# Two edits of a one-core encoder layer: a tail whose last quarter is centred early and summed by TensorE, and an attention head scaled by POOL

## The chip, the cores and the metric

The kernel runs on one core of one Trainium2 chip. The metric is the device time of one execution in microseconds (us). A core has five engines that this text names: PE (TensorE, matmuls into PSUM), DVE (VectorE, elementwise work), ACT (ScalarE, activations, with a free scale, bias and row sum), POOL (GpSimd, elementwise work from SBUF to SBUF, and DMAs of its own queue) and SP (a queue that issues DMAs). Each engine executes its own list of instructions in order and waits on semaphores for the others. POOL cannot read PSUM.

## The reference, cut to what matters

One layer on 1024 prompt rows and 32 sample rows, 1024 features. The parts that the change touches are the softmax of the sparse attention, and the second layer norm.

```python
logits = jnp.where(valid[:, :, None, None, :], logits + bias, NEG)
p = jax.nn.softmax(logits, axis=-1)
out = jnp.einsum('btgrk,btkgd->btgrd', p, v_sel)
...
hid = jax.nn.relu(x @ w_ff1)
ff = (hid * hid) @ w_ff2
x = _layernorm(ALPHA * x + ff, ln2_g, ln2_b)

def _layernorm(x, g, b):
    mu = jnp.mean(xf, axis=-1, keepdims=True)
    xc = xf - mu
    var = jnp.mean(xc * xc, axis=-1, keepdims=True)
    y = xc * lax.rsqrt(var + LN_EPS) * g + b
```

## The kernel before, in words

Everything is held with features on the 128 partitions and rows of x (1056 of them) along the free dimension. A product of two f32 matrices is made of three matmuls on a high and a low part (lines 875 to 877 in the feed-forward part, 131 to 133 elsewhere), so every weight tile is loaded, split by ACT (L108, high part) and POOL or DVE (L111, low part), and then multiplied. The order of a run is: input projections, indexer scores and the top-k search; attention and the output projection (about 350 to 545 us of the profile); first layer norm and feed-forward products by a Strassen-like scheme (seven products instead of eight, on halves of 528 rows); the last of these products, the second layer norm, and the output.

**Attention.** `PLAN` lists nine query tiles `t` of 128 rows (one of 32), each with four pairs of heads `g2`. For a pair, `att_softmax` multiplies queries with keys and adds the position bias (L572 to L576, PE), adds the mask and takes the row minimum of the negated logits on DVE (L578, one instruction for each chunk of up to 512 keys, each followed by a read of the accumulator), joins the minima of two chunks (L583, DVE), takes the exponential with its row sum (L584, ACT), the reciprocal (L586, DVE), and scales the two heads: head 0 by DVE (L587), head 1 by ACT (L588). `att_values` then transposes the result in tiles of 128 (L606, PE) and multiplies with the values (L620 to L623). Six `L` tiles let three pairs be under way. POOL meanwhile makes low parts of weights (`whl`, L111) and of attention outputs (`area`, L111), and issues the loads of the queries `q` (L521), each of which waits until PE has read the buffer it writes. Other jobs, such as parts of the output projection and of the first layer norm, are put between the pairs. A scheduler decides the order on every engine in this stage.

**The tail.** From the feed-forward part on the order is written out by hand: `run` goes through a list of `Step`s and emits for each its loads, preparations, matmuls (`mm`) and what follows (`post`), on all engines in that order. A `plain` step is 12 matmuls (four weight tiles, three matmuls each) into one PSUM tile, and one DVE addition of it to a tile of z (L1288). A quarter `q` of the rows (264) has eight plain steps, one for each feature tile `d`. `M5` and `M3` are steps of two of the seven products. The order of the end is `qs[0] + qs[1] + M5 + M3[0] + qs[2] + M3[1] + qs[3]`. Four PSUM tiles `acc` rotate through all of these. Ahead of `qs[0]` stand the steps `P4`, whose four results are added to z by DVE (L1028), and 12 `fold`s (L1035) add kept partial sums `u` to z, eight on DVE and four on POOL.

**Second layer norm.** The quarters 0 to 2 go through `ln2_parts`: three sums over tiles on POOL (L1254), the mean by a matmul with a matrix of 1/1024 (`small_sum`, L1233; one such f32 call is two MATMUL records in the trace), centring on DVE (L1262), squares on ACT (L1264, L1267) and their sums on POOL (L1268), the root (L1273, ACT) and its reciprocal (L1274, DVE), scaling of the four z tiles (L1239) by the engine that the table at the end names, and scale and shift on ACT with the store (L1244, L1245). The last quarter has its own function, `last_quarter`: after two plain steps it takes a rough offset (`offset`, a sum over two tiles), subtracts it from each tile (L1305, tiles 0 to 3 on DVE after their product, 4 to 7 on POOL before it), squares each tile (L1310, ACT), and keeps two running sums, of the tiles and of the squares, on DVE (L1312 and L1313, each 128 x 264). At the end PE forms mean and variance of these sums (L1233), and the tiles are centred exactly (L1341, DVE and POOL), scaled (L1239, three on DVE and one on POOL), finished on ACT (L1244) and stored.

## Time and profile before

| | |
|---|---|
| median of 3 runs | 1309.21 us (1307.82 to 4234.3) |
| the profiled execution | 1309.35 us |
| its span, first to last instruction | 1307.0 us |
| PE busy | 1231.6 us, 94% |
| DVE busy | 963.6 us, 74% |
| ACT busy | 694.1 us, 53% |
| POOL busy | 584.0 us, 45% |

The span is the time between the first and the last instruction in the trace, and the profiled execution's own time is 2.35 us above it. The page gives for each engine how long it was busy, the chain of work that ended last, and the costliest groups of instructions. In the views that are used here, "idle" before an instruction is the time in which its engine had nothing to do just before it, with the instruction that ended the wait behind an arrow. Matmuls overlap, so the distance from one start to the next tells their cost and not their length. PEclk is the clock that TensorE was granted, where 1.00 is the full one.

### The profile page before, as it was taken

Reading aid. Unit: us, or ns where it says so; the run is one execution under the profiler, and the core shown is the slowest. Engines: PE = TensorE matmul, PEld = TensorE weight load, DVE = VectorE, ACT = ScalarE, POOL = GpSimd, SP = SyncE. Lnnn points to the kernel's source line nnn. Section 1 sums busy time; section 2 is a strip of 40 time slices with the busy share of each in tenths; the row PEclk is TensorE's granted clock in tenths of the full one; section 3 lists DMA queues with packets and bytes.
Section 4 is the critical chain, followed back from the end, with each engine's and each line's share of the span. In section 5 each row is a group of like instructions: output and inputs, shape, how many; then the busy total and the mean of one; then the engine's idle time right before and its main releaser. Section 6 shows DMA issues by size and latency. Waiting matters only on the chain. (4 is left out here: it accounts for less than half of the span.)

```text
span 1307.0 us, 24077 instructions
## 1 busy us (share of the span) xinstructions
PE 1231.6 (94%) x8846; PEld 1194.1 (91%) x8846; DVE 963.6 (74%) x1986; ACT 694.1 (53%) x1370; POOL 584.0 (45%) x463
## 2 busy tenths in 40 slices
PE   7999999998899998799799999999899999998994
PEld 6999999988898987788799999999899999998993
DVE  5675799999579988877857667576647667577666
ACT  5666989843698888784322222221344444444244
POOL 2412355423521252374544453544444444448764
PEclk9999999998999999999899999999999999999996
DMA  6321111125631231243134344443873563553112
GB/s 207 100 72 38 34 49 50 49 100 168 172 89 20 49 73 33 65 157 122 43 124 161 119 157 147 143 164 126 283 276 93 178 203 108 163 170 118 34 51 84
DMA packets 97222, 149.98 MB, mean 115 GB/s; under 512 B 12456, under 2 KB 41808, under 8 KB 97104
## 3 DMA queue, kind: packets, MB, share of 16 engines
q1 hardware_dynamic: 81664, 139.55, 32.9%
q0 software_dynamic: 9504, 4.33, 2.0%
q10 hardware_dynamic: 5936, 4.58, 1.2%
q8 instruction: 69, 1.13, 0.4%
q14 instruction: 49, 0.40, 0.1%
HBM read 105.41 MB, written 43.00 MB: 114 GB/s over the span
## 5 line engine op out<-in xcount | busy, mean ns | idle before, releaser
L111 POOL TENSOR_TENSOR whl<-wraw,whl 128x512 fp32r<-128x512 f32 (+1 forms) x184 | 253.5, 1382 | 413.1 <-ACT whl L108 391.1
L875 PE MATMUL acc<-b,whl 128*128 128x264 f32 x1088 | 310.0, 285 | 5.8 <-DVE ring L954 2.7
L876 PE MATMUL acc<-b,whl 128*128 128x264 f32 x1088 | 310.1, 285 | 0.0
L877 PE MATMUL acc<-b,whl 128*128 128x264 f32 x1088 | 308.6, 284 | 0.0
L875 PEld LDWEIGHTS acc<-b,whl 128*128 128x128 f32 x1088 | 204.8, 188 | 6.8 <-DVE ring L954 2.9
L108 ACT ACTIVATE whl<-wraw 128x512 fp32r<-128x512 f32 (+1 forms) x184 | 113.4, 623 | 174.2 <-DVE wraw L870 141.9
L877 PEld LDWEIGHTS acc<-b,whl 128*128 128x128 f32 x1088 | 205.4, 189 | 0.0
L876 PEld LDWEIGHTS acc<-b,whl 128*128 128x128 f32 x1088 | 204.4, 188 | 0.0
L132 PE MATMUL mm<-area,whl 128*128 128x384 f32 (+4 forms) x552 | 180.6, 328 | 0.4 <-DVE area L111 0.4
L131 PE MATMUL mm<-xh,whl 128*128 128x384 f32 (+4 forms) x520 | 170.4, 329 | 9.6 <-ACT whl L108 5.6
L133 PE MATMUL mm<-xh,whl 128*128 128x384 f32 (+4 forms) x520 | 169.2, 330 | 0.4 <-POOL whl L111 0.4
L111 DVE TENSOR_TENSOR b<-xraw,b 128x528 fp32r<-128x528 f32 x94 | 69.9, 745 | 85.3 <-ACT b L108 85.2
L108 ACT ACTIVATE b<-xraw 128x528 fp32r<-128x528 f32 x94 | 60.6, 644 | 132.5 <-PE acc L877 75.0
L441 ACT ACTIVATE junka<-s,cand 128x1024 bf16<-128x1024 f32 (+1 forms) x93 | 96.4, 1036 | 31.0 <-DVE cand L454 25.5
L131 PEld LDWEIGHTS mm<-xh,whl 128*128 128x128 f32 (+1 forms) x520 | 97.1, 187 | 12.5 <-ACT whl L108 6.2
L132 PEld LDWEIGHTS mm<-area,whl 128*128 128x128 f32 (+1 forms) x552 | 103.2, 187 | 3.3 <-DVE area L111 0.8
L133 PEld LDWEIGHTS mm<-xh,whl 128*128 128x128 f32 (+1 forms) x520 | 96.9, 187 | 3.8 <-POOL whl L111 1.3
L111 POOL TENSOR_TENSOR whl<-at,whl 128x512 fp32r<-128x512 f32 x56 | 80.4, 1445 | 31.8 <-ACT whl L108 31.8
L443 DVE TENSOR_SCALAR_CACHE_REDUCE junk<-s,cand 128x384 bf16<-128x384 f32 (+1 forms) x124 | 80.2, 647 | 1.1
L875 PE MATMUL acc<-area,whl 128*128 128x264 f32 x240 | 68.6, 286 | 0.0
L877 PE MATMUL acc<-area,whl 128*128 128x264 f32 x240 | 68.1, 284 | 0.0
L876 PE MATMUL acc<-area,whl 128*128 128x264 f32 x240 | 68.0, 283 | 0.0
(323 smaller groups left out, 3327.4 us busy)
## 6 DMA issues: line engine op xcount, KB each, us to landing
hd<-ring SPq DMA_DIRECT2D x98, 264.0 KB, 2.1
xraw<-hd SPq DMA_DIRECT2D x98, 264.0 KB, 2.7
at<-in_w_dram SPq DMA_DIRECT2D x58, 256.0 KB, 3.5
wraw<-in_win_dram SPq DMA_DIRECT2D x52, 256.0 KB, 2.6
wraw<-in_wo_dram SPq DMA_DIRECT2D x40, 256.0 KB, 2.7
w_a<-in_w_dram SPq DMA_DIRECT2D x23, 256.0 KB, 3.6
w_c<-in_w_dram SPq DMA_DIRECT2D x19, 256.0 KB, 3.7
zz<-zd SPq DMA_DIRECT2D x4, 1056.0 KB, 8.7
```

What stands on the lines that cost most here:

```text
L108: S.activation(hi, raw, AF.Copy)
L111: (lo_eng or G).tensor_tensor(lo, raw, f32(hi), op=OP.subtract)
L131: PE.matmul(ps, wh[k], a, start=(k == 0), stop=False)
L132: PE.matmul(ps, wh[k], b, start=False, stop=False)
L133: PE.matmul(ps, wl[k], a, start=False, stop=(k == K - 1))
L441: S.activation(junk(R, N), s, AF.Sign, bias=c, scale=-1.0, accum_out=cnt[:R, i:i + 1])
L443: V.tensor_scalar(junk(R, N), s, c, -float(k), op0=OP.is_ge, op1=OP.add, accum_out=cnt[:R, i:i + 1])
L875: PE.matmul(ps, wh, xhi, start=start, stop=False, skip_group_check=more)
L876: PE.matmul(ps, wh, xlo, start=False, stop=False, skip_group_check=more)
L877: PE.matmul(ps, wl, xhi, start=False, stop=stop, skip_group_check=more)
```

## The change

In `att_softmax` the minimum of the second chunk starts from that of the first, so that the joining instruction goes away, and head 0 is scaled by POOL instead of DVE. In the tail, all folds go to DVE, and six of them move from `P4` into the first six steps of `qs[0]`. `last_quarter` takes its offset from tiles 4 and 5 ahead of its own products, after step 6 of `qs[2]`, and DVE subtracts it from all eight tiles, two at a time, between there and the end of `M3[1]`. DVE keeps running sums of the tiles 0 to 3 alone; PE adds these sums and each of the tiles 4 to 7 with its square into a PSUM tile `stats` (`total`, one step later than the tile, the last two after step 7). At the end DVE alone scales, and it also finishes the last two tiles. The scaling of quarter 2 goes from POOL to DVE, and its last two outputs stand behind the exact centring. The parts of quarter 1's norm stand one to four steps earlier.

```diff
@@ -575,16 +575,16 @@
                     PE.matmul(ps[:R, w - 256:w], antir[:, :R], hh[g][:, h0 + i, :], start=False, stop=False)
                     mm = PE.matmul(ps[:R, w - 256:w], antir[:, :R], hl[g][:, h0 + i, :], start=False, stop=True)
                 done["QK"] = mm
-                V.tensor_tensor_reduce(L[:, c:c + n], ps[:R, pad:pad + n], mask[:, c:c + n], -1.0, -LOWEST,
-                                       op0=OP.add, op1=OP.min, accum_out=mn[:R, i, ci:ci + 1])
+                V.tensor_tensor_reduce(L[:, c:c + n], ps[:R, pad:pad + n], mask[:, c:c + n], -1.0,
+                                       mn[:R, i, 0:1] if ci else -LOWEST, op0=OP.add, op1=OP.min,
+                                       accum_out=mn[:R, i, ci:ci + 1])
         sm = small.tile([128, 2], F32, name="sm")
         for h in range(2):
-            if len(chunks) == 2:
-                V.tensor_scalar(mn[:R, h, 0:1], mn[:R, h, 0:1], mn[:R, h, 1:2], None, op0=OP.min)
-            S.activation(ls[h], ls[h], AF.Exp, bias=mn[:R, h, 0:1], scale=-1.0, accum_out=sm[:R, h:h + 1])
+            S.activation(ls[h], ls[h], AF.Exp, bias=mn[:R, h, len(chunks) - 1:len(chunks)], scale=-1.0,
+                         accum_out=sm[:R, h:h + 1])
         rs = small.tile([128, 2], F32, name="rs")
         V.reciprocal(rs[:R], sm[:R])
-        V.tensor_scalar(ls[0], ls[0], rs[:R, 0:1], None, op0=OP.mult)
+        G.tensor_scalar(ls[0], ls[0], rs[:R, 0:1], None, op0=OP.mult)
         S.activation(ls[1], ls[1], AF.Copy, scale=rs[:R, 1:2])
         return ls
 
@@ -1291,7 +1291,9 @@
     def plain(q):
         return [plain_step(q, d) for d in range(8)]
 
-    def last_quarter():
+    last_out = []
+
+    def last_quarter(qs, M3):
 
         c0, n = H + Q, Q
         cols = slice(c0, c0 + n)
@@ -1301,58 +1303,68 @@
         def ztile(d):
             return z[d // 2][:, d % 2, cols]
 
-        def centre(d, e):
-            e.tensor_tensor(ztile(d), ztile(d), got["off"], op=OP.add)
+        def offset():
+            mid = small_sum([(ones, z[2][:, a, cols]) for a in range(2)])
+            got["off"] = n2_ring.parts[0][:, :Q]
+            S.activation(got["off"], mid, AF.Copy, scale=-4.0)
+
+        def centre(i):
+            zi = z[i][:, :, cols]
+            V.tensor_tensor(zi, zi, got["off"][:, None].to_broadcast([128, 2, n]), op=OP.add)
 
         def square(d):
-            sq = got["sq"] = unit("sqa" if d % 2 else "sqb")[:, 0]
+            sq = got[d] = n2_ring.parts[1 + d % 4][:, :Q]
+            if d == 0:
+                got["sums"] = unit("s1")
             sums = got["sums"]
             S.activation(sums[:, 1] if d == 0 else sq, ztile(d), AF.Square)
-            if 0 < d < 7:
+            if 0 < d < 4:
                 V.tensor_tensor(sums[:, 0], ztile(0) if d == 1 else sums[:, 0], ztile(d), op=OP.add)
                 V.tensor_tensor(sums[:, 1], sums[:, 1], sq, op=OP.add)
 
-        def offset():
-            mid = small_sum([(ones, z[0][:, a, cols]) for a in range(2)])
-            got["off"] = n2_ring.parts[0][:, :Q]
-            S.activation(got["off"], mid, AF.Copy, scale=-4.0)
-            for i in range(4, 8):
-                centre(i, G)
-
-        def begin(*ds):
-            if ds[0] == 0:
-                got["sums"] = unit("s1")
-            for i in ds:
-                centre(i, V)
-                square(i)
+        def total(d):
+
+            if d == 3:
+                got["stats"] = new_acc()
+            for i, a in enumerate((got["sums"][:, 0], got["sums"][:, 1]) if d == 3 else (ztile(d), got[d])):
+                PE.matmul(got["stats"][:, i], ones, a, start=(d == 3), stop=(d == 7))
 
         def end():
-            sums = got["sums"]
-            mean = small_sum([(ones, sums[:, 0]), (ones, ztile(7))])
-            var = small_sum([(ones, sums[:, 1]), (ones, got["sq"])])
+            mean, var = got["stats"][:, 0], got["stats"][:, 1]
             mean2 = unit("s2")[:, 0]
             S.activation(mean2, mean, AF.Square)
             pair = unit("rstd")
             mean1, rstd = pair[:, 0], pair[:, 1]
+            V.tensor_tensor(mean2, var, mean2, op=OP.subtract)
             S.activation(mean1, mean, AF.Copy)
-            for i in range(4):
+            S.activation(rstd, mean2, AF.Sqrt, bias=eps)
+            for i in (0, 2, 3, 1):
                 zi = z[i][:, :, cols]
                 e, m = (V, mean) if i < 2 else (G, mean1)
                 e.tensor_tensor(zi, zi, m[:, None].to_broadcast([128, 2, n]), op=OP.subtract)
                 if i == 0:
-                    V.tensor_tensor(mean2, var, mean2, op=OP.subtract)
-                    S.activation(rstd, mean2, AF.Sqrt, bias=eps)
-                if i == 1:
                     V.reciprocal(rstd, rstd)
-            for i, e in ((0, V), (3, G), (1, V), (2, V)):
-                scaled(c0, n, rstd, (i,), e)
-                out(c0, n, (i,))
-
-        steps[1].post.append(offset)
-        steps[2].post.append(lambda: begin(0, 1))
-        steps[3].post.append(lambda: begin(2, 3))
-        for d in range(4, 8):
+            for f in last_out:
+                f()
+            for i in range(4):
+                scaled(c0, n, rstd, (i,), V)
+                zi = z[i][:, :, cols]
+                for a in range(2):
+                    j = 2 * i + a
+                    g, b = lnw[:, 2, j:j + 1], lnw[:, 3, j:j + 1]
+                    if i < 3:
+                        S.activation(zi[:, a], zi[:, a], AF.Identity, scale=g, bias=b)
+                    else:
+                        V.tensor_scalar(zi[:, a], zi[:, a], g, b, op0=OP.mult, op1=OP.add)
+                    nc.sync.dma_start(yT[j * 128:j * 128 + 128, c0:c0 + n], zi[:, a])
+
+        for f, st in ((offset, qs[2][6]), (lambda: centre(2), qs[2][7]), (lambda: centre(3), M3[1][0]),
+                      (lambda: centre(0), M3[1][1]), (lambda: centre(1), M3[1][3])):
+            st.post.append(f)
+        for d in range(8):
             steps[d].post.append(lambda d=d: square(d))
+        for d in range(3, 8):
+            steps[min(d + 1, 7)].post.append(lambda d=d: total(d))
         steps[7].post.append(end)
         return steps
 
@@ -1372,14 +1384,16 @@
         steps[n + 36 + 4 * j].prep.append(prep)
     for j in range(4):
         d = (j + 3) % 4
-        P4[j].post[:0] = [fold(d, 1, 0, V), fold(d, 1, 1, G)]
-    qs = [plain(0), plain(1), plain(2), last_quarter()]
-    P4[0].post.append(fold(3, 0, 1, V))
+        P4[j].post[:0] = [fold(d, 1, 0, V)]
+    qs = [plain(0), plain(1), plain(2)]
+    P4[0].post += [fold(3, m, 1, V) for m in range(2)]
     for d in range(3):
-        P4[1 + d].post.insert(0, fold(d, 0, 1, V))
+        for m in range(2):
+            qs[0][2 * d + m].post.append(fold(d, m, 1, V))
     (load5, _, prep5, step5), (load3, make3, prep3, step3) = P5, P3
     M5 = [step5(d, (0, 1)) for d in range(4)]
     M3 = [[step3(d, (c,)) for d in range(4)] for c in range(2)]
+    qs.append(last_quarter(qs, M3))
     steps += qs[0] + qs[1] + M5 + M3[0] + qs[2] + M3[1] + qs[3]
     for j in range(4):
         if j < 3:
@@ -1394,11 +1408,14 @@
     for f, st in zip(prep3, (M5[3], M3[0][0], M3[0][1])):
         st.prep.append(f)
     for q, eng, when in ((0, G, (qs[1][2], qs[1][7], M5[3], M3[0][0], M3[0][0], M3[0][1], M3[0][2], M3[0][3])),
-                         (1, V, (M3[0][1], qs[2][5], M3[1][0], M3[1][2], M3[1][1], M3[1][2], M3[1][3], qs[3][0])),
-                         (2, G, (M3[1][1], qs[3][3], qs[3][4], qs[3][5], qs[3][5], qs[3][6], qs[3][6], qs[3][7]))):
+                         (1, V, (M3[0][1], qs[2][3], qs[2][4], qs[2][6], qs[2][6], qs[2][7], M3[1][0], M3[1][1])),
+                         (2, V, (M3[1][1], qs[3][3], qs[3][4], qs[3][5], qs[3][5], qs[3][6], None, None))):
         when = (qs[q][3], qs[q][5], qs[q][7]) + when
         for f, st in zip(ln2_parts(q * Q, Q, eng), when):
-            st.post.append(f)
+            if st is None:
+                last_out.append(f)
+            else:
+                st.post.append(f)
     with tc.manual_schedule(engines=ORDERED):
         run(steps, 3, 6)
```

Two places show how the instructions stand; names carry a buffer number behind an underscore. On DVE, in the last plain steps, from the reciprocal of quarter 2 to the last step's addition (L1288 adds a plain product, L1312 and L1313 are the running sums; zz0 to zz3 hold z, two tiles each). Before:

```order
L1274 RECIPROCAL at_7307<-at_7307 128x264
L1288 TENSOR_TENSOR zz2_10751<-acc_14352,zz2_10751 128x264
L1312 TENSOR_TENSOR w_d_11223<-w_d_11223,zz2_10751 128x264
L1313 TENSOR_TENSOR w_d_11223<-w_d_11223,at_7307 128x264
L1288 TENSOR_TENSOR zz2_10751<-acc_14371,zz2_10751 128x264
L1312 TENSOR_TENSOR w_d_11223<-w_d_11223,zz2_10751 128x264
L1313 TENSOR_TENSOR w_d_11223<-w_d_11223 128x264
L1288 TENSOR_TENSOR zz3_10783<-acc_14394,zz3_10783 128x264
L1312 TENSOR_TENSOR w_d_11223<-w_d_11223,zz3_10783 128x264
L1313 TENSOR_TENSOR w_d_11223<-w_d_11223,at_7307 128x264
L1288 TENSOR_TENSOR zz3_10783<-acc_14419,zz3_10783 128x264
```

The same stretch in the change, up to the last quarter's reciprocal (L1239 scales quarter 2, L1338 is the variance, L1344 the exact centring):

```order
L1274 RECIPROCAL at_7275<-at_7275 128x264
L1288 TENSOR_TENSOR zz2_10719<-acc_14316,zz2_10719 128x264
L1239 TENSOR_TENSOR zz0_10419<-zz0_10419,at_7275 128x2x264
L1239 TENSOR_TENSOR zz1_10452<-zz1_10452,at_7275 128x2x264
L1288 TENSOR_TENSOR zz2_10719<-acc_14336,zz2_10719 128x264
L1239 TENSOR_TENSOR zz2_10719<-zz2_10719,at_7275 128x2x264
L1239 TENSOR_TENSOR zz3_10751<-zz3_10751,at_7275 128x2x264
L1288 TENSOR_TENSOR zz3_10751<-acc_14359,zz3_10751 128x264
L1288 TENSOR_TENSOR zz3_10751<-acc_14380,zz3_10751 128x264
L1338 TENSOR_TENSOR w_d_11191<-acc_14331,w_d_11191 128x264
L1344 TENSOR_TENSOR zz0_10419<-zz0_10419,acc_14331 128x2x264
L1346 RECIPROCAL at_7275<-at_7275 128x264
```

The running sums between the additions are gone, and the four scalings of quarter 2, which POOL did, stand there. On POOL, a stretch of the attention stage around tile 2 (`area` is the low part of an attention output). Before:

```order
L521 DMA q_5368<-qd_2596 128x4x128
L521 DMA q_5554<-qd_2596 128x4x128
L111 TENSOR_TENSOR area_63<-ao_4478,area_63 128x2x128 x2
L521 DMA q_5729<-qd_2596 128x4x128
L111 TENSOR_TENSOR area_63<-ao_5044,area_63 128x2x32 x2
L521 DMA q_5907<-qd_2596 128x4x128
L111 TENSOR_TENSOR whl_5535<-wraw_5536,whl_5535 128x512
L111 TENSOR_TENSOR whl_5624<-wraw_5625,whl_5624 128x512
```

And in the change, where the same loads `q_5729`, `q_5907` are named `q_5701`, `q_5875`:

```order
L111 TENSOR_TENSOR area_63<-ao_4468,area_63 128x2x128
L587 TENSOR_SCALAR L_5172<-L_5172,rs_5197 128x768
L521 DMA q_5701<-qd_2596 128x4x128
L587 TENSOR_SCALAR L_5261<-L_5261,rs_5286 128x768
L111 TENSOR_TENSOR area_63<-ao_5028,area_63 128x2x32 x2
L587 TENSOR_SCALAR L_5351<-L_5351,rs_5376 128x768
L521 DMA q_5875<-qd_2596 128x4x128
L111 TENSOR_TENSOR whl_5511<-wraw_5512,whl_5511 128x512
L587 TENSOR_SCALAR L_5441<-L_5441,rs_5466 128x768
L111 TENSOR_TENSOR whl_5598<-wraw_5599,whl_5598 128x512
```

The scalings (L587) stand among the splits, and behind and ahead of loads that wait for PE, where POOL had only splits and loads. Of the folds, eight stand on DVE between the last two groups of L1028 before; in the change six do, and the other six stand one by one behind the first six additions L1288 of `qs[0]`, and none on POOL.

## Rows read from the trace of the kernel before

**Rows 1.** Page, part 1: busy time, share of the span, instructions.

```profile
PE 1231.6 (94%) x8846; PEld 1194.1 (91%) x8846; DVE 963.6 (74%) x1986; ACT 694.1 (53%) x1370; POOL 584.0 (45%) x463
```

**Rows 2.** Chain that ended last, its end: start us, us, what.

```profile
1266.89 0.90 PE acc L1233 x4
...
1291.54 3.90 PE acc L1233 x8
1295.46 0.43 DVE w_d L1343
...
1296.51 1.79 DVE at L1346
...
1302.32 1.99 ACT zz L1244 x4
```

**Rows 3.** Timeline of PE in the last plain steps: start, us, instruction, idle before.

```profile
1270.53 0.28 PE L875 MATMUL acc<-area,ew 128*128 128x264 f32 x1
...
1278.34 1.05 PE L1233 MATMUL acc<-w_d,cs 128*128 128x264 f32 x4
...
1284.94 0.28 PE L877 MATMUL acc<-area,ew 128*128 128x264 f32 x1
```

**Rows 4.** Timeline of DVE, ACT and POOL from 1284 us to the end.

```profile
1284.74 5.64 POOL L1239 TENSOR_TENSOR zz<-zz,at 128x528 f32<-128x528 f32 x4 [5.39 <-DVE at L1274]
...
1286.26 1.52 DVE L1313 TENSOR_TENSOR w_d<-w_d,at 128x264 f32<-128x264 f32 x1
...
1291.56 0.43 DVE L1313 TENSOR_TENSOR w_d<-w_d,at 128x264 f32<-128x264 f32 x1
1291.91 0.43 DVE L1288 TENSOR_TENSOR zz<-acc,zz 128x264 f32<-128x264 f32 x1
...
1293.43 0.41 ACT L1310 ACTIVATE w_d<-zz 128x264 f32<-128x264 f32 x1
...
1298.32 0.71 DVE L1239 TENSOR_TENSOR zz<-zz,at 128x528 f32<-128x528 f32 x1
```

**Rows 5.** Timeline of DVE at the folds, and of PE behind them.

```profile
1193.41 3.52 DVE L1035 TENSOR_TENSOR zz<-zz,w_c 128x528 f32<-128x528 f32 x2
1196.86 9.36 DVE L1035 TENSOR_TENSOR zz<-zz,w_b 128x528 f32<-128x528 f32 x6
1206.14 2.54 DVE L1028 TENSOR_TENSOR zz<-acc,zz 128x528 f32<-128x528 f32 x4
...
1206.88 0.39 PE L875 MATMUL acc<-area,ew 128*128 128x264 f32 x1 [3.41 <-DVE zz L1028]
```

**Rows 6.** Attention stage: busy time of all engines, then of L587, of L583.

```profile
350.00:545.00 195.00, 181.88 (x1226) 169.66 (x1225) 162.01 (x498) 163.88 (x368) 65.43 (x62) 0.98 0.25 62
...
350.00:545.00 195.00, 22.25 (x36) 0.98 0.25 62
...
350.00:545.00 195.00, 6.66 (x32) 0.98 0.25 62
```

**Rows 7.** Attention stage, waits of PE: us in total, times, longest.

```profile
PE qk_b L572 <- DVE mn L578: 5.7, 6, 2.8
PE tr_b L606 <- ACT L L588: 1.8, 1, 1.8
PE mm_b L131 <- DVE z L414: 1.8, 1, 1.8
PE tr_b L606 <- DVE L L587: 1.3, 1, 1.3
PE tr_b L606 <- DVE pt L614: 1.2, 3, 0.5
```

**Rows 8.** Groups by shape: busy us, mean ns of one, idle before.

```profile
L587 DVE TENSOR_SCALAR L<-L,rs 128x1024 f32<-128x1024 f32 x4 | 3.0, 751 | 0.1
...
L111 POOL TENSOR_TENSOR whl<-wraw,whl 128x512 fp32r<-128x512 f32 x182 | 251.9, 1389 | 405.8 <-ACT whl L108 383.8 <-PE qk L274 14.8 <-issue 4.1
...
L405 POOL CAST area<-ch 128x384 fp32r<-128x384 f32 x4 | 2.5, 646 | 4.4 <-PE mm L132 4.4
```

## The prediction, as it was made before the change ran

> **What bounds the kernel now.** I read the page's busy shares first. [rows 1] say that PE is busy for 94% of the span and no other engine for more than 74%. So a cut on DVE, ACT or POOL is worth something only where PE stands still for it, and the two edits have to be priced by PE's idle time in their own stages. Next I read the end of the chain of waits [rows 2], because at the end of a run PE has nothing left and every engine's delay is on the path. The reader is to see there that nothing but the sums (L1233), DVE's centring and reciprocal and ACT's scale and shift follows the products, and that the four last sums took 3.90 us where two others took 0.90, that is twice as long for each. The timelines of PE [rows 3] and of the other engines [rows 4] then show why the end starts late. The first product of `qs[3]` starts at 1270.53, which I call T0, the last one at 1284.94, but the sums wait until 1291.54, 6.5 us in which PE does nothing. DVE is the engine that is late: the addition of the last tile starts at 1291.91 because the running sums ahead of it are slow. One of them took 1.52 us at 1286.26, while POOL scaled quarter 2 (5.64 us from 1284.74), and 0.43 us at 1291.56, when POOL was still.
>
> For the fold edit I read the timelines of DVE and PE at the folds [rows 5]. Eight folds take 12.9 us on DVE, the additions of `P4` stand behind them, and PE's first plain product waits 3.41 us for one of these additions. For the attention edit I read the stage by engine [rows 6] and PE's waits in it [rows 7]: of 195 us PE is busy for 181.88, DVE for 162.01, ACT for 163.88 and POOL for 65.43. Its waits on DVE come to 5.7 + 1.8 + 1.3 + 1.2 = 10.0 us, 5.7 of them at the row minima (L578), and one wait of 1.8 on ACT's scaling.
>
> **The tail.** *Removed:* the offset's sum within `qs[3]`, six of DVE's twelve running sums, POOL's part in the scaling, and the four sums after the last addition. *Added:* five pairs of sums on PE, three of them among the plain steps, two after the last. A plain step is 12 matmuls of 0.12 us, 1.46 us, so eight are 11.7 us ([rows 3]: 14.5 us from T0 to the end of the last, with the offset's sum, a sum of quarter 2 and the waits between). A pair of f32 sums is 0.90 us at the full clock, from the x4 row of [rows 2]. The products of `qs[3]` then end at 11.7 + 0.9 (quarter 2's sum) + 3 x 0.9 = T0 + 15.3. The last addition is 0.43 us and ACT's square 0.41 [rows 4]: T0 + 16.1. Tile 6's sums lie under these; tile 7's take 0.9 more: T0 + 17.0. I take full clock here because PE now stands still for under a microsecond before them, where it stood for 6.5 us before; at the half clock they take another 0.9, and I keep that as a bound. Subtraction 0.43 [rows 2], the root and the reciprocal: the chain before has 0.43 at 1295.46 and the reciprocal's end at 1298.30, which is 2.84 us from one to the other with the centring between. The change keeps this order, so the scaling starts at T0 + 19.9. DVE then does two pieces of work of 0.7 us [rows 4] (centring tile pair 1, scaling pair 0), ACT starts at T0 + 21.3 on six outputs of 0.5 us (1.99 for four in [rows 2]) and ends at T0 + 24.3. Beside it DVE has five such pieces and two outputs of about 0.43, which end at T0 + 24.3 too; POOL's centring of the pairs 2 and 3 lies beside the reciprocal, and quarter 2's four moved outputs (2.0 us on ACT) between the root and T0 + 21.3. From ACT's last output (1302.32 + 1.99) to the end of the span, 1307.0, are 2.7 us, the stores, which stay. That makes T0 + 27.0, against 1307.0 - 1270.53 = 36.5 before: **9.5 us**, of which I keep 9.2, since ACT and DVE end together and either may hold the other up a little.
>
> T0 itself moves. The offset's sum goes ahead of it: +0.9. Its subtractions on DVE (0.7 us each, four) lie between PE's products of `qs[2]` and `M3[1]`, in which nothing of DVE is late by more than four PSUM tiles allow; I cost them at nothing, and they cost up to 0.7 each if that cover is gone. Six folds in the place of eight take six times the mean of the row, 9.36 / 6 = 1.56, 9.4 us in all: 12.88 - 9.4 = 3.5 us less ahead of the additions. The first addition could then start at 1206.14 - 3.5 = 1202.6, but PE's own work ends at 1206.88 - 3.41 = 1203.47 only, and PE went on 0.74 us after that addition's start: of the 3.41, 0.8 stay: -2.6. The six moved folds go behind DVE's additions of `qs[0]`, one for each 1.46 us step. With POOL at work beside them DVE's 0.43 + 1.56 = 1.99 us exceed the step by 0.53; over six steps that is 3.2 us of delay at most, which the four PSUM tiles (5.8 us of PE) absorb. **Tail in all: -9.2 + 0.9 - 2.6 = -10.9 us**, with the bounds -7 (half clock, and folds that give nothing) and -11.5.
>
> **Attention.** *Removed from DVE:* 36 scalings, 22.25 us, and 32 minimum joins, 6.66 us [rows 6], 28.9 of its 162 us, or 0.8 us for each of the 36 pairs of heads. *Added to POOL:* 36 scalings over 19,072 elements a partition in all (four each of 1024, 896, 768, 640, 512, 384, 256, 128 and 160 keys). The trace of before has no such instruction on POOL, so I bound it. The nearest one-input row is the CAST of [rows 8], 646 ns for 384, or 1.68 ns an element: 32 us. The two-input split, 1389 ns for 512 or 2.71 ns an element, gives 51.7 us. POOL then stands at 97 to 117 us of 195, so it isn't the bound on average. A scaling of 1024 keys takes 1.7 to 2.8 us, against 0.75 on DVE [rows 8]. It lies between the exponential and the transposes of a pair, while PE multiplies the queries of later pairs; with three pairs under way, only one of the 36 pairs had PE wait for DVE's scaling (1.3 us [rows 7]). I take the one-input rate, because a multiplication by one value per partition reads one tile.
>
> What goes for sure is DVE's 0.8 us ahead of the row minima. In [rows 7] six waits there make 5.7 us, the longest 2.8. The five others average 0.6, less than the 0.8 taken away, so they go (2.9) and the longest shrinks by 0.8: 3.7. I take **-4 us**. All of PE's waits on DVE and the one on ACT, 11.8 us, bound it on one side. On the other, POOL's excess, 51.7 - 22.25 = 29 us, all of it waited for, bounds it.
>
> The sum against the profiled run, 1309.35, is -14.9; the median is 0.14 below that run. 1309.2 - 14.9 = **1294 us**.
>
> **The rivals.** (a) *Attention gives nothing*, because PE's waits come back at POOL's scaling: a scaling 1 us longer in a stage in which POOL's queue also has loads that wait for PE. For it speaks that ACT's busy time (163.88) is untouched and stands above DVE's; against it that the waits of PE on ACT are 1.8 us only. Time 1309.2 - 10.9 = 1298. (b) *All of PE's waits on DVE go*: 1309.2 - 10.9 - 12 = 1286. For it speaks that 10.0 of the 11.8 us wait for the one engine that loses work; against it that ACT, at 163.88 us of 195, is loaded as DVE was and would end the next wait. (c) *The tail gives half*: the change moves the waits of DVE behind the folds into `qs[0]`, or the sums run at the half clock, and attention gives nothing: 1309.2 - 5 = 1304. (d) *Slower: POOL's scaling is on the path.* Its place is the transposes L606. At the two-input rate each pair's scaling takes up to 2 us longer than DVE's, and POOL, with splits of 1.39 us and loads that wait for PE ahead of it, executes in order. The tail pays for 10.9 us, so it decides from 0.3 us of new PE waiting a pair; with all of the excess it is 1309.2 - 10.9 + 29 = 1327. Against it: POOL is idle for two thirds of the stage [rows 6], and no wait of PE for POOL is among the five longest [rows 7].
>
> The Trainium skill, "GPSIMD Engine Reference", section "Engine selection", speaks against this edit: it names VectorE for elementwise work, with GPSIMD about twice as slow for two inputs, and adds that one input is roughly line-rate. No run here shows a POOL scaling yet. By its factor of two on DVE's 22.25 us the added work would be 44.5 us, (d)'s excess 22 and its time 1320; by its line-rate, an estimate at the page's clock of 1.2 GHz, it would be 16 us, and (d) could not be. The row of the CAST, 1.68 ns an element, lies between the two.
>
> **How the numbers follow.** Forecast 0.40, (a) 0.25, (b) 0.15, (c) 0.10, (d) 0.10. The likeliest case's own range is 1289 to 1299, from the tail's bounds and 3 us either way in attention, whose whole order the change deals anew. The range that should hold 8 of 10 leaves out most of (d) and the far half of (b): 1282 to 1307. A measurement of this kernel can tell about 2%, 26 us, from no change. Faster by that is under 1283, half of (b) and a little more: 0.08. Slower by that is over 1335, past (d)'s full price, so it needs a second loss: 0.03. Within: 0.89.
>
> **What would show it.** Tail: PE's sums right behind the last product, with no idle time of 6 us, the reciprocal of the last quarter done 20 us after T0 instead of 27.8, and DVE's additions there at 0.43 us. Folds: PE's wait at the first plain product under 1 us. Attention: PE's waits at L572 on L578 near 2 us, L587 on POOL at 1.7 us for 1024 keys, PE's waits at L606 on it under 2 us. The prediction is wrong if PE's waits at L606 on POOL pass 6 us, if POOL's scaling is nearer 2.8 us, or if DVE's folds in `qs[0]` hold PE's next PSUM tile.

## The result, and the profile after

The changed kernel takes 1297.05 us (median of 4 runs, 1296.6 to 1297.86) against 1308.51 us for the kernel before in the same group of runs: a ratio of 0.991, with a 95% interval from 0.9894 to 0.9926 (one of the four runs of the kernel before took 4234.3 us; the other three lie between 1307.72 and 1309.21). Run again later as e5, it gave 1298.95 us and 0.9922 (0.9907 to 0.9938). So it is 10 to 12 us faster. That is under 1%, less than the 2% that the prediction held to be the least that can be told, but both intervals leave out 1. The forecast was 1294 us in a range from 1282 to 1307. By the experiments below the gain comes from the tail, and the prediction's term for attention was not there.

The profiled run of the change has a span of 1295.3 us. Busy times, to be laid beside [rows 1]:

```profile
PE 1231.1 (95%) x8858; PEld 1193.2 (92%) x8858; DVE 943.1 (73%) x1923; ACT 693.1 (54%) x1368; POOL 620.7 (48%) x486
```

PE does as much as before in 11.7 us less. To see where they went I take, in each trace, the starts of matmuls that both kernels have, and split the span at them (times in us; "attention" is from the first L572 to the last L622, "gap" from there to the first L875, "folds" from the 1301st L875 to the first plain product, "plain" from there to the last plain product, "end" from there to the end of the span):

| kernel | attention | gap | folds | plain | end | span |
|---|---|---|---|---|---|---|
| before | 203.54 | 93.74 | 78.21 | 78.06 | 22.11 | 1307.0 |
| change | 202.63 | 94.34 | 74.64 | 79.97 | 14.14 | 1295.3 |
| change again (e5) | 203.92 | 95.35 | 74.64 | 80.12 | 13.96 | 1300.4 |

The last three stretches repeat to 0.2 us, the attention stage and the gap behind it move by one or two us from one profile to the next of the same kernel. The runs of one kernel also scatter with TensorE's mean granted clock: the slowest of e5, 1302.15 us, has 0.982 and the fastest, 1296.93 us, 0.988. In the first profile of the change the folds give 3.6 us, the end gives 8.0, the plain steps take 1.9 back: 9.6 us. The rest of the 11.7 lies in stretches ahead of the folds that vary by as much.

The end, in the chain that ended last (start, us, what), stands against [rows 2]:

```profile
1281.41 1.79 PE acc L1330 x8
1283.29 0.40 ACT w_d L1335
1283.71 0.44 DVE w_d L1338
1284.18 0.40 ACT at L1339
1284.60 0.70 DVE zz L1344
1285.31 1.71 DVE at L1346
1287.02 0.56 DVE zz L1344
1287.58 0.62 DVE zz L1239
1288.23 1.25 ACT zz L1356 x3
```

The reader is to see that the last four sums follow the last product (its start is 1281.13) at once and take 1.79 us, where four took 3.90 us before. The granted clock is 1.00 in these 1.79 us, the upper of its two levels, and was 0.50 in those 3.90, the lower one, behind 6.5 us in which PE stood still. Behind them ACT and DVE take turns: the square of the mean (L1335), the variance (L1338), the copy of the mean (L1339) and the first centring (L1344) all stand ahead of the reciprocal (L1346), which ends at 1287.02.

The timeline of the last outputs (start, us, instruction, idle time before it) goes on from there:

```profile
1287.49 2.55 DVE L1239 TENSOR_TENSOR zz<-zz,at 128x528 f32<-128x528 f32 x4
1288.23 3.10 ACT L1356 ACTIVATE zz<-zz,lnw 128x264 f32<-128x264 f32 x6 [1.27 <-DVE zz L1239]
1288.86 4.00 SPq L1359 DMA_DIRECT2D out_dram<-zz  x8
1290.08 0.74 DVE L1358 TENSOR_SCALAR zz<-zz,lnw 128x264 f32<-128x264 f32 x2
```

Two engines now make outputs, ACT until 1291.32 and DVE until 1290.82, but SP issues the eight stores one after the other, 0.5 us each, until 1292.86. The span ends 2.4 us after that.

The attention stage, busy time of all engines in the same 195 us as in [rows 6] (PE, PEld, DVE, ACT, POOL), then POOL's scalings alone:

```profile
350.00:545.00 195.00, 182.54 (x1227) 168.67 (x1227) 143.98 (x430) 162.84 (x366) 122.15 (x97) 0.99 0.23 59
...
350.00:545.00 195.00, 58.32 (x36) 0.99 0.23 59
```

DVE is rid of 18.0 us of busy time and not of 28.9, the sum of what went. POOL takes 58.3 us for what cost DVE 22.25. One row by shape (busy us, mean ns, idle before) gives its rate:

```profile
L587 POOL TENSOR_SCALAR L<-L,rs 128x1024 f32<-128x1024 f32 x4 | 11.5, 2883 | 7.2 <-DVE rs L586 7.1
L587 POOL TENSOR_SCALAR L<-L,rs 128x384 f32<-128x384 f32 x4 | 5.0, 1248 | 10.4 <-DVE rs L586 10.3
```

2883 ns for 1024 elements are 2.8 ns each, and 1248 for 384 are 3.2, twice the CAST's 646 ns for 384 in [rows 8]: the upper bound of the prediction, and a little more. And yet PE's waits in the stage (us in total, times, longest) show no wait for it, to be compared with [rows 7]:

```profile
PE qk_b L572 <- DVE mn L578: 8.3, 9, 3.7
...
PE tr_b L606 <- DVE pt L614: 1.1, 2, 0.6
PE mm_b L131 <- DVE z L414: 1.0, 1, 1.0
```

PE's wait for the row minima has grown from 5.7 to 8.3 us, although DVE has less to do; other traces with the same attention code have 6.5 (e2, e5) and 6.7 (e4).

The gap behind the stage, which neither [rows 7] nor the prediction covers, holds PE's longest single wait of these two stretches, for an addition on DVE in the first feed-forward products. Before and after the change:

```profile
PE mm L131 <- DVE xraw L815: 6.2, 1, 6.2
PE mm L131 <- DVE xraw L815: 7.7, 1, 7.7
```

It is 7.7 in e2 and e5 too, 6.1 in e1, 4.3 in e3, 4.5 in e12 and 3.9 in e4, though none of the edits touches the code around it. So a microsecond or two that the attention stage wins can be lost or doubled here.

### The profile page after: what moved, and what is told of

The parts are those of the page before. It is cut to its first block, busy times and chain, and to the rows that moved or that the text cites. A ratio compares the mean times of both kernels' runs of the same rounds, so it can differ in the third digit from the quotient of the medians.

```text
span 1295.3 us, 24166 instructions
## 1 busy us (share of the span) xinstructions
PE 1231.1 (95%) x8858; PEld 1193.2 (92%) x8858; DVE 943.1 (73%) x1923; ACT 693.1 (54%) x1368; POOL 620.7 (48%) x486
## 5 line engine op out<-in xcount | busy, mean ns | idle before, releaser
L875 PE MATMUL acc<-b,whl 128*128 128x264 f32 x1088 | 310.0, 285 | 5.4 <-DVE ring L954 2.3
L875 PEld LDWEIGHTS acc<-b,whl 128*128 128x128 f32 x1088 | 204.8, 188 | 6.5 <-DVE ring L954 2.5
L587 POOL TENSOR_SCALAR L<-L,rs 128x1024 f32<-128x1024 f32 (+8 forms) x36 | 58.3, 1621 | 38.5 <-DVE rs L586 36.4
L875 PE MATMUL acc<-area,whl 128*128 128x264 f32 x240 | 68.6, 286 | 0.0
L877 PE MATMUL acc<-area,whl 128*128 128x264 f32 x240 | 68.2, 284 | 0.0
```

Source lines behind the costliest of these rows:

```text
L587: G.tensor_scalar(ls[0], ls[0], rs[:R, 0:1], None, op0=OP.mult)
L875: PE.matmul(ps, wh, xhi, start=start, stop=False, skip_group_check=more)
L877: PE.matmul(ps, wl, xhi, start=False, stop=stop, skip_group_check=more)
```

## The experiments

Twelve kernels ran in three groups of four, each beside runs of the kernel before. Times are medians, ratios are against the kernel before of the group.

**e1, the tail alone.** The attention part of the diff is undone (`V.tensor_tensor_reduce` with -LOWEST, the joining instruction, and `V.tensor_scalar` for head 0).

> The change with the attention stage put back as it was before: only the tail is edited. The traces give the tail 3.5 us at the folds, 8.0 us behind the last product, and 1.9 us back for the sums among the plain steps, 9.6 us in all: 1298.9 us (ratio 0.9927). By the prediction's terms (tail -10.9, attention -4) it would be 1297.6. If attention gave nothing, it equals the change, 1297.0; if moving the scaling to POOL cost time and the tail paid for it, it is faster than the change, under 1295.

Measured: 1297.68 us, ratio 0.9916 (0.9901 to 0.9931). It is as fast as the change (0.991 and 0.9922). Its trace has folds 74.64, plain 80.11, end 14.45, the change's within half a microsecond.

**e2, the attention alone.**

```diff
-        V.tensor_scalar(ls[0], ls[0], rs[:R, 0:1], None, op0=OP.mult)
+        G.tensor_scalar(ls[0], ls[0], rs[:R, 0:1], None, op0=OP.mult)
```

together with the chained minimum, on the kernel before.

> The kernel before with the attention edits alone. By the prediction's term of -4 it is 1304.5 us. By the traces, in which the stage's last product came 0.9 us earlier against its first (and 0.4 to 0.6 us went back right behind it), 1307 to 1308. If POOL's longer scaling were on the path it would be over 1309.

Measured: 1310.42 us, ratio 1.0017 (1.0006 to 1.0028). The -4 us of the prediction is refuted, and by itself the edit is rather a loss of 1 to 4 us. Its trace, which is of the fastest of its twelve runs (1307.88), shows 201.58 us in attention, 2 less than before, and 95.83 in the gap behind, 2 more; 1.5 of these 2 are the wait for L815.

**e3, only the chained minimum of the attention edits.**

```diff
-        G.tensor_scalar(ls[0], ls[0], rs[:R, 0:1], None, op0=OP.mult)
+        V.tensor_scalar(ls[0], ls[0], rs[:R, 0:1], None, op0=OP.mult)
```

> The change with head 0 scaled by DVE as before, so that of the attention edits only the chained minimum is left (DVE is rid of 6.7 us instead of 28.9). If DVE's work in the stage is what PE waits for, this lies between e1 and the change, nearer e1 (by 6.7/28.9 of the way). If POOL's scaling (2.9 us for 1024 keys against 0.75 on DVE) costs as much as DVE's relief brings, it is equal to or faster than the change by up to 2 us.

Measured: 1300.76 us, ratio 0.994 (0.9927 to 0.9952). Neither answer: it is slower than e1 by 3 us, with 205.88 us in attention, and not between e1 and the change. The row of all engines in the stage tells one thing all the same:

```profile
350.00:545.00 195.00, 180.68 (x1219) 167.46 (x1219) 160.54 (x463) 162.89 (x364) 62.16 (x61) 0.99 0.24 58
```

DVE is busy for 160.54 us against 162.01, though 6.66 us of instructions (L583) are gone. Those were 0.2 us each, and most of that lay under their neighbours. What the scaling then takes off DVE is 160.54 - 143.98 = 16.6 us, not 22.25. The busy times of DVE over the whole run, which no window cuts, say the same: 961.7 us in e1, 959.7 in e3, 943.1 in the change. A sum of durations overstates what an engine is relieved of.

**e4, the folds as before.**

```diff
-        P4[j].post[:0] = [fold(d, 1, 0, V)]
+        P4[j].post[:0] = [fold(d, 1, 0, V), fold(d, 1, 1, G)]
...
-    P4[0].post += [fold(3, m, 1, V) for m in range(2)]
+    P4[0].post.append(fold(3, 0, 1, V))
     for d in range(3):
-        for m in range(2):
-            qs[0][2 * d + m].post.append(fold(d, m, 1, V))
+        P4[1 + d].post.insert(0, fold(d, 0, 1, V))
```

> The change with the folds as before: eight on DVE and four on POOL ahead of the additions of P4. By the traces PE's wait of 3.4 us at the first plain product comes back: 1300.5 us (ratio to before 0.9939). The prediction priced this at 2.6 us: 1299.6. If the moved folds cost as much in the plain steps as they save, it is equal to the change, 1297.0.

Measured: 1302.55 us, ratio 0.9953 (0.9937 to 0.9969), 3.6 to 5.5 us above the change's two medians and 4.9 above e1 in the same group. Its nine runs spread from 1297.22 to 1305.76, and the trace is of the fastest, whose whole span (1295.4) is no longer than the change's because its gap is 3 us shorter; only its last stretches can be compared. There the folds stretch is 78.20 again, as before, the plain steps take 79.60, and the wait is back (PE's waits from 1190 us on):

```profile
PE acc L875 <- DVE zz L1028: 3.4, 1, 3.4
```

In the change the same question has another answer, the whole of what is left, at 1224.72:

```profile
PE acc L875 <- DVE zz L1288: 0.6, 1, 0.6
```

So the folds give 3.57 us where they were and cost 0.4 to 0.5 in the plain steps, about as much as this wait. That is shown. DVE's six folds ahead of the additions, the additions, and the first moved fold, in the timeline of the change (start, us for all of the row), answer to [rows 5]:

```profile
1191.25 4.14 DVE L1035 TENSOR_TENSOR zz<-zz,w_c 128x528 f32<-128x528 f32 x3
1195.32 3.04 DVE L1035 TENSOR_TENSOR zz<-zz,w_b 128x528 f32<-128x528 f32 x3
1199.15 2.91 DVE L1028 TENSOR_TENSOR zz<-acc,zz 128x528 f32<-128x528 f32 x4 [0.79 <-PE acc L877]
...
1203.17 0.70 DVE L1035 TENSOR_TENSOR zz<-zz,w_b 128x528 f32<-128x528 f32 x1
```

The six take 7.2 us, 1.2 us each, where the eight took 1.6 each. One by one they take either 0.70 or 1.80 us: in the change three of the six are long, beside POOL's splits, and three short, in the 2.0 us from 1194.21 on in which POOL stands still; before, seven of the eight were long, beside POOL's folds and splits. Of the six moved ones five take 0.70, with POOL still, and one 0.98.

**e5, the change again.**

> The change itself, once more, beside the three kernels of this group and as a yardstick for the first four: 1297.1 us was its median before. Every theory expects 1296 to 1299; a median above 1299.5 would say that the difference to e1 and e3 lies within what the same kernel does from one group of runs to the next.

Measured: 1298.95 us, ratio 0.9922 (0.9907 to 0.9938), above the change's first median by 1.9 us. Differences of 2 us between kernels of different groups say nothing.

**e6, POOL scales twice.**

```diff
         G.tensor_scalar(ls[0], ls[0], rs[:R, 0:1], None, op0=OP.mult)
+        G.tensor_scalar(ls[0], ls[0], rs[:R, 0:1], None, op0=OP.mult)
```

> The change with head 0 scaled by POOL twice, one after the other (its values are then off by that factor), so POOL has another 58 us in the attention stage, about 180 of 195. If POOL's scaling lay on the path (rival d), PE would wait for most of the 58 us: 1340 or more. If three pairs under way cover it, the first 1.6 us a pair are covered too and the time grows by PE's waits at L606 only: 1297 to 1307.

Measured: 1327.24 us, ratio 1.0138 (1.0118 to 1.0158), 28 us above e5. Half of the added 58 us is on the path: between the two answers, nearer the first. Attention takes 226.97 us and the gap 99.81. Two rows of PE's waits up to 580 us (its lines after the edit are one higher, so L588 is POOL's second scaling):

```profile
PE pv_b L623 <- DVE ao L629: 7.3, 3, 3.8
...
PE tr_b L607 <- POOL L L588: 1.1, 3, 0.6
```

The cost hardly shows as a wait of PE for POOL. It comes through the others: DVE's row minima, for one, wait 11.3 us for PE's transposes, which need the scaled heads, and waited 2.9 in e5. How the rest of the 28 us comes about was not followed. Rival (d) named the right place to be afraid of: one scaling a pair is covered, two are not.

**e7, the reciprocal of the first layer norm behind two row minima.** In the trace of the change the longest wait of PE in the stage, 3.67 us before 495.39, ends with a row minimum. DVE and ACT ahead of it:

```profile
490.54 0.17 DVE L586 RECIPROCAL rs<-sm 128x2 f32<-128x2 f32 x1 [0.39 <-ACT L L583]
492.97 1.95 DVE L687 RECIPROCAL rstd<-rstd 128x288 f32<-128x288 f32 x1 [2.26 <-ACT rstd L686]
494.84 0.49 DVE L578 CUSTOM_DVE_ANT_0 L<-qk_b,s 128x384 f32<-128x384 f32 x1
```

```profile
491.14 1.28 ACT L686 ACT_TABLE_LOAD   x1
492.44 0.50 ACT L686 ACTIVATE rstd<-st_b,eps 128x288 f32<-128x288 f32 x1
```

DVE waits 2.26 us for ACT's root, which needs 1.28 us to load its table, takes 1.95 us for the reciprocal, and only then comes to the minimum. In the kernel before one of the two minima stood ahead of that reciprocal. The edit puts both ahead and nothing else:

```diff
-    (3, ("l20", "l21", "l22", "")),
-    (2, ("w10", "w11", "w12", "")),
+    (3, ("l20", "l21", "", "")),
+    (2, ("w10", "l22v w11", "w12", "")),
...
-                    with tc.issue_after(done["QK"].ins):
+                    with tc.issue_after(done["MN" if name[3:] == "v" else "QK"].ins):
```

> The change with one swap on DVE: the reciprocal L687 of the first layer norm behind the two row minima L578 that it stood ahead of. In the trace of the change DVE stands still there for 2.3 us because ACT's root L686 is late, and PE waits 3.7 us for the minima behind it. If DVE's place in the order and not its load is what costs the attention stage its gain, PE's wait of 3.7 us falls under 1 us and the run to about 1294. If another engine ends the next wait, it stays at 1297.

Measured: 1296.57 us, ratio 0.9903 (0.9887 to 0.9918), against 1298.95 and 0.9922 of e5 in the same group: 2.4 us less, with intervals that overlap, so by itself no difference that can be told (e12 comes back to it). PE's waits at L572 in its trace:

```profile
492.88 0.44 PE L572 MATMUL qk_b<-kh,q 128*128 128x384 f32 x1 [0.66 <-DVE mn L578]
501.72 0.69 PE L572 MATMUL qk_b<-kh,q 128*128 128x384 f32 x1 [3.07 <-DVE mn L578]
```

The wait of 3.67 us is down to 0.66, as expected of the order, and one pair later stands another of 3.07, because the scaling of the layer norm (L690) has come to lie ahead of the next two minima on DVE, and itself stands behind a reciprocal that waited for ACT's exponential (now L583):

```profile
498.06 0.17 DVE L586 RECIPROCAL rs<-sm 128x2 f32<-128x2 f32 x1 [1.19 <-ACT L L583]
498.14 3.05 DVE L690 TENSOR_TENSOR z<-z,rstd 128x576 f32<-128x576 f32 x4
501.11 0.54 DVE L578 CUSTOM_DVE_ANT_0 L<-qk_b,s 128x384 f32<-128x384 f32 x1
```

The wait moved on. The longest of the kernel before, 2.82 us ahead of 498.53, stood behind the same four scalings, and so does the second longest of the change (1.78 us ahead of 500.01). DVE, before and then after:

```profile
494.25 3.29 DVE L690 TENSOR_TENSOR z<-z,rstd 128x576 f32<-128x576 f32 x4
...
497.93 0.53 DVE L578 CUSTOM_DVE_ANT_0 L<-qk_b,s 128x384 f32<-128x384 f32 x1
```

```profile
496.67 2.75 DVE L690 TENSOR_TENSOR z<-z,rstd 128x576 f32<-128x576 f32 x4
...
499.41 0.53 DVE L578 CUSTOM_DVE_ANT_0 L<-qk_b,s 128x384 f32<-128x384 f32 x1
```

**e8, quarter 2 scaled by DVE in the kernel before.** `(2, G, (M3[1][1], ...` becomes `(2, V, (M3[1][1], ...`.

> The kernel before with one letter changed: quarter 2 is scaled by DVE instead of POOL, everything else as before. If DVE's running sums are slow because POOL scales beside them, they fall from 1.5 to 0.43 us, four scalings of 0.7 us come onto DVE, and the last sums start about 3 us sooner: 1305 us. If DVE's amount of work is the cause, they start later by 2.8 us: 1311.

Measured: 1308.51 us, ratio 0.9991 (0.9977 to 1.0005), no difference. Both halves of the expectation are there and cancel. In its trace the running sums are quick:

```profile
1290.33 0.43 DVE L1312 TENSOR_TENSOR w_d<-w_d,zz 128x264 f32<-128x264 f32 x1
1290.85 0.43 DVE L1313 TENSOR_TENSOR w_d<-w_d,at 128x264 f32<-128x264 f32 x1
1291.20 0.43 DVE L1288 TENSOR_TENSOR zz<-acc,zz 128x264 f32<-128x264 f32 x1
```

Yet the last addition starts 6.0 us after the last product's start (1285.17) against 7.0 before, since DVE has the four scalings instead. The end is 21.27 us against 22.11. So POOL's scaling beside DVE was not what the tail could be cured of alone; DVE had too much behind the last product, and the change takes the running sums of four tiles, and the centrings, away from there.

**e9, four stores instead of eight, and e10, the root first.**

```diff
-                    nc.sync.dma_start(yT[j * 128:j * 128 + 128, c0:c0 + n], zi[:, a])
+            for i in (0, 1, 3, 2):
+                nc.sync.dma_start(yT[i * 256:i * 256 + 256, c0:c0 + n].rearrange("(a p) n -> p a n", a=2),
+                                  z[i][:, :, cols])
```

> The change with the last quarter's eight stores put into four of two tiles each, the pair that DVE finishes ahead of the last one of ACT. In the trace of the change SP issues the eight one after the other, 0.5 us each, until 1292.9, 1.5 us after ACT's last output. If this queue ends the run, the last issue ends 1.0 us sooner and the time from the last plain product to the end falls from 14.1 to about 13.1 us. If the transfers themselves do (they carry twice as much each), it stays or grows. The whole run moves by less than its spread, so the trace decides.

Measured: 1300.0 us, ratio 0.9926 (0.9909 to 0.9943); end 14.97 us, longer by 0.8. The queue was relieved (its row, beside the eight of 4.00 us above):

```profile
1291.58 2.50 SPq L1360 DMA_DIRECT2D out_dram<-zz  x4
```

Issuing ends at 1294.08, 0.5 us after ACT's last output instead of 1.5, but the span ends at 1298.3, 4.2 us later instead of 2.4. The larger stores take longer to land (median 2.8 us from issue against 2.0). The queue alone does not set the end.

```diff
-            S.activation(mean1, mean, AF.Copy)
             S.activation(rstd, mean2, AF.Sqrt, bias=eps)
+            S.activation(mean1, mean, AF.Copy)
+            V.reciprocal(rstd, rstd)
...
             for i in range(4):
+                if i < 2:
+                    exact(i)
                 scaled(c0, n, rstd, (i,), V)
```

(`exact` is the centring of a pair, which stood ahead; POOL's two stay ahead.)

> The change with the root ahead of the copy of the mean on ACT, and the reciprocal ahead of the first exact centring on DVE. In the trace of the change the copy (0.39 us) stands between variance and root, and the centring (0.70) between root and reciprocal. If these two are what the prediction missed behind the sums, the reciprocal is done 0.5 us sooner after the last product and the first output starts 0.5 us sooner; the end moves by 0.5 us, or by nothing if the store queue ends the run.

Measured: 1299.02 us, ratio 0.9921 (0.9905 to 0.9938); end 14.85 us. DVE's rows:

```profile
1287.81 1.80 DVE L1341 RECIPROCAL at<-at 128x264 f32<-128x264 f32 x1 [0.58 <-ACT at L1339]
...
1290.21 1.04 DVE L1239 TENSOR_TENSOR zz<-zz,at 128x528 f32<-128x528 f32 x1
```

The reciprocal is done 5.3 us after the first of the last four sums (1284.34) instead of 5.8, as expected, but the first scaling now falls beside POOL's centring and takes 1.04 us, and the first output starts 6.9 us after those sums, where it was 7.0. The half microsecond is given back at once, and the end is no shorter.

**e11 and e12, both edits,** on e1's kernel and on e7's.

> Both of the last two edits on the tail edits alone (attention as in the kernel before). From the last plain product to the end 12.6 us if both are worth what is said of them (1.0 and 0.5), and 1296 us as a whole. If the attention edits are worth nothing, it equals the next one.

> Both edits on the change with the reciprocal of the first layer norm moved as in e7. 12.6 us from the last plain product to the end, and about 1295 us as a whole if the attention edits give the 1 to 2 us that the traces show.

Measured: e11 1299.4 us, ratio 0.9927 (0.991 to 0.9944), end 15.57; e12 1296.92 us, ratio 0.9898 (0.9881 to 0.9914), end 15.14. Both ends are longer than the change's 14.14, so both expectations fail there, and the two tail edits together shorten nothing. But e12 is not equal to e11, as it should be if the attention edits with e7's swap were worth nothing: it is 2.5 us faster, and five of its six runs lie below all 18 runs of e9, e10 and e11. With e7 against e5 that makes two groups in which the kernel with the swap is 2 to 3 us ahead, and both traces have the shortest gap, 90.73 us. This is a sign and not proof: the ratios' intervals overlap or touch, e12 differs from each of its neighbours by more than the swap, the change itself did not run in that group, and e4 has a gap of 91.33 without it. No version is shown to be better than the change; this one would be the first to run again.

## Why the prediction was right, and where it was not

**Right in sign and range,** with 1297 to 1299 us in 1282 to 1307 and the tail as the source. Point by point:

*The folds* were to give 2.6 us and gave 3.57 less 0.4 to 0.5 in the plain steps. The mis-sized term is the 0.8 us of PE's wait that was to stay. I let the first addition start only where PE's own work ends; in the change it starts at 1199.15, 2.0 us ahead of the first plain product (1201.16), and PE waits for nothing there at all. The mean fold was off too, 1.2 us for six and 0.70 for most of the moved ones where I took 1.56, but the 3.5 us that I took off ahead of the additions were already more than the wait of 3.41.

*The plain steps* were to take back 1.7 us: 0.8 within the last quarter (15.3 against 14.5) and 0.9 for the offset's sum ahead of it. In e4, whose folds are the old ones, they take 79.60 - 78.06 = 1.5 us more. That is as forecast. The offset's subtractions, costed at nothing, cost nothing: from 1190 us on PE waits only for the 0.6 us at 1224.72, long before them.

*The end* was to fall from 22 to about 12 us from the last product's start and fell to 14.1; the reciprocal is done 21.1 us after T0 (1265.95 in the change), where I had put 20. The sums themselves ran at the full clock, as I chose. Two terms were too small. From the last sum to the end of the reciprocal I took 2.84 us from the rows of before; there the mean was summed first and its square and copy lay under the variance's sums. In the change mean and variance are ready together, and the chain takes 1287.02 - 1283.2 = 3.8 us. From ACT's last output to the end I took 2.7 us; it is 3.9, as SP's issues, 0.5 us each, now lag behind two engines that make outputs. The first follows from the rows; e10 shows that undoing it alone brings nothing, as the next wait takes its place. For the second e9 shows that the issuing can be shortened and the landing then grows; which of the two would end the run with other sizes stays open.

*Attention* is the step that failed: "The five others average 0.6, less than the 0.8 taken away, so they go". They did not go. e2 by itself is 0.1 to 0.3% slower, e1 without the edit is as fast as the change, and the stage takes 200.7 to 203.5 us in the four traces without the edits (before, e1, e8, e11) and 201.2 to 203.9 in the six with both of them and the layer norm in its place (change, e2, e4, e5, e9, e10). Rival (a), attention gives nothing, 1298 us, is what happened, and its reason holds in part: PE's waits come back, though not at the scaling. Three things were wrong. DVE lost 18 us and not 28.9 (e3). PE's long waits for a row minimum follow less from how much DVE has to do than from what stands ahead of the minimum in DVE's list: in all three traces looked at, it is the first layer norm, either its four scalings (2.82 us before, 1.78 in the change, 3.07 in e7) or its reciprocal waiting for ACT's root (3.67 in the change), and none of that is lighter in the change. The prediction took the 2.8 us from [rows 7] without asking what stood ahead of that minimum. In e7 the longest wait was taken away, and another came one pair later. And POOL's rate is the upper bound, which the prediction had named as a sign of its being wrong: 2.88 us for 1024 keys, where it put 1.7. PE's waits at L572, which were to be near 2 us, are 6.5 to 8.3 (change, e2, e4, e5). Rival (d) had the price nearly right, 58.3 us for 51.7, and its place was covered once (no wait of PE for POOL) and not twice (e6, 28 of 58 us).

*What was luck.* The point forecast is off by 3 to 5 us, 4 of them attention and 2 the end, with 0.5 too little for the folds on the other side. In the first profile another 2.1 us come from stretches that neither edit is priced in, which brought it nearer than its terms were.

The rule of the Trainium skill's page "GPSIMD Engine Reference", section "Engine selection", is that elementwise work belongs on VectorE and that one input is roughly at line rate on GPSIMD. The first half agrees with the rows, 58.3 us on POOL for what cost DVE 22.25. The second does not: at 2.8 ns an element the 19,072 elements cost more than three times the 16 us that the prediction estimated from that rate, and the measurement decides.

What stays open: why e3 is 3 us slower than e1. It differs by the chained minimum and by the order that the scheduler makes of the whole stage, and these were not separated. Nor did a kernel run with POOL's scaling and without the chained minimum: that the two edits cancel, the one costing what the other gives, is a rival to attention giving nothing, and no run rules it out.

## What to carry to other kernels

Price relief for an engine by the busy time that its window loses and not by a sum of durations, and only where the profile shows the bottleneck engine waiting for that engine's amount of work; if it waits for one instruction that stands behind another job in that engine's list, less load elsewhere may change nothing. At the end of a kernel, list everything between the last matmul and the last store on every queue, in its new order: a link that lay under another before is on the path as soon as that other goes. A slower engine may take over work as long as the buffers cover it once; double it in an experiment to see how near the edge is.

## What the runs showed of the hardware

A multiplication by one value per partition, f32, takes POOL 2.8 to 3.2 ns an element at 1024 to 384 elements (2883 and 1248 ns), as its two-input split does (1389 ns for 512). DVE's two-input instructions of 128x264, both from SBUF, take 0.43 us where POOL is still and 1.07 to 1.52 us beside POOL's scalings; those of 128x528 (the folds) take 0.70 us where POOL is still and 1.8 beside POOL's two-input instructions. DVE's additions of 128x264 out of PSUM (L1288) take 0.42 us on average in the stretch of the last plain steps of both traces, before and e8.
